# Queries and keys of the dilated attention by seven half-size products, its operands re-made in two forms, and its attention steps paced by hand

## The chip, the cores and the metric

The kernel runs on one core of one Trainium2 chip. The metric is the device time of one execution in microseconds, the median of three runs. PE is TensorE, DVE VectorE, ACT ScalarE, POOL GpSimd; SP is the sequencer whose queue issues most of the loads.

## The reference

One sequence of 512 tokens, width 1024, float32, goes through two layers and a final RMSNorm. Layer 0 attends in a window, layer 1 in three dilated groups of a window each; a SwiGLU feed-forward follows each attention. The change lies in layer 1:

```python
def dilated_mixture_attention(h, w_qkv, w_out):
    b, s, _ = h.shape
    qkv = (h @ w_qkv).reshape(b, s, N_GROUPS_B, 3, H_B, HEAD_DIM)      # 3 groups, q k v, 16 heads of 64
    slopes = alibi_slopes(H_B)[:, None]
    outs, lses = [], []
    for gi, (win, dil) in enumerate(DILATED_GROUPS):                    # (128,1), (512,4), (2048,16)
        q = to_residue(qkv[:, :, gi, 0], dil)[:, :, :, None]
        k = to_residue(qkv[:, :, gi, 1], dil)
        v = to_residue(qkv[:, :, gi, 2], dil)
        o, lse = banded_attention(q, k, v, slopes, dil, win // (2 * dil), BLOCK_B)
        outs.append(from_residue(o[:, :, :, 0], b, dil))
        lses.append(from_residue(lse[:, :, :, 0], b, dil))
    wts = jax.nn.softmax(jnp.stack(lses), axis=0)
    o = jnp.einsum('gbsh,gbshd->bshd', wts, jnp.stack(outs).astype(jnp.float32))
    return o.astype(h.dtype).reshape(b, s, H_B * HEAD_DIM) @ w_out

def reference(x, ...):
    for i in range(DEPTH):                                              # 2
        h = rmsnorm(x, norm_mix[i])
        x = x + (window_gqa_sink(h, ...) if i % 2 == 0 else dilated_mixture_attention(h, ...))
        h = rmsnorm(x, norm_ffn[i])
        x = x + swiglu(h, w_gate[i], w_up[i], w_down[i])
    return rmsnorm(x, norm_final)
```

## The kernel before

Activations lie transposed: `x` has 8 chunks of 128 features by 512 tokens. Every float32 operand of a product is kept as a high part (a copy rounded by ACT) and a low part (source less high part, by DVE), and a product is three matmuls: high by high, high by low, low by high (`mm3`, line 121). All matmuls of the dense parts move 256 columns against a 128x128 stationary block. "Step" is used here for six such matmuls, the unit in which the work is dealt out.

The two feed-forwards (`swiglu`, from line 601) compute most of their products in a Strassen-Winograd form already: a pair of weight blocks is combined into seven half-size products (`product`, line 737; `strassen`, line 744). Their weight sums are made by DMAs that add while they load (`load_sums`, line 690: two plain loads by SP, then two accumulating loads issued by POOL), two DVE additions and five splits.

The second attention (from line 1075) works on eight pairs of heads, p = 0 to 7.

- `qk_units` (line 1086) makes the queries and the keys of pair p in group g: two units of 8 steps each (`unit`, line 204). A unit loads one block of 128x1024 weights, splits it (ACT line 97, DVE line 98), runs 48 matmuls over all 512 tokens into one PSUM bank and leaves it scaled by DVE (`q_done` line 1093, `k_done` line 1107). The RMSNorm's row factor `rb` is applied here. For the first group the result is put from class order to token order, and split again for exact scores.
- `v_unit` (line 1121) makes the values of two pairs at a time: 16 steps (`values`, line 229). The values of group 0 for all pairs are made first, against `oh, ol`, which hold the input in token order; the rest runs against `xh, xl`, in class order.
- Per pair: `scores_a` (line 1139) for group 0 in two halves, with the reductions on DVE and the exponentials on ACT; `merge` (line 1281) takes the row statistics through DRAM into class order; `turn_a` (line 1173) transposes the weights on PE; then, in one go, `finish(p-1)` (the weighing of groups 1 and 2 of the pair before), `weigh_a`, and `scores_b` (line 1205) of groups 1 and 2; then exponentials (ACT), normalisation (DVE, and POOL line 1248), `turn_b` (line 1251) and `merge_rows` (line 1294).
- PE's order is written by hand: `attention_a` and `attention_b` give steps with waits between them, counted in the steps of a line of filling units (`fillers`, line 1377), and `spread` (line 169) deals them out. The order on DVE, ACT, POOL and SP in this stage is the planner's, which places instructions by program order, by readiness and by its own costs. Each engine then runs its list strictly in that order. Buffers of a tag rotate (`wraw`, `wh`, `wl`: 3 each, PSUM `mm`: 3, `sc`: 2, `tp`: 2, `ov`: 1), and a later tile of a tag waits for the last reader of the tile whose place it takes.

One filling line between two pairs holds 64 steps: six units of 8 and one `v_unit` of 16.

Of the kernel before, what the change touches and what calls it, by code (L numbers as in the profile page):

```python
# [53 lines left out]
def q_scales():  # L54

    s = np.zeros((128, 16), np.float32)
    for p in range(2):
        for i in range(4):
            for hf in range(2):
                s[64 * hf:64 * hf + 64, 4 * p + i] = 0.125 / SLOPES[8 * p + 4 * hf + i]  # L60
    for p in range(8):
        for hf in range(2):
            s[64 * hf:64 * hf + 64, 8 + p] = 0.125 / SLOPES[2 * p + hf]
    return s


def trunk(ctx, tc, xT, gains, sink, tabs, qsc, wunits, wv, outT, outR):
# [13 lines left out]
    x = const.tile([128, NK, S], F32, name="x")  # L81
    qs_sb = const.tile([128, 16], F32, name="qs_sb")
# [50 lines left out]
    def split_queries(q, pair):  # L133
        for a, (own, other) in enumerate((HALVES, HALVES[::-1])):
# [3 lines left out]
    def split_keys(k, pair, low):  # L138
        for a, (own, other) in enumerate((HALVES, HALVES[::-1])):
# [935 lines left out]
    with tc.tile_pool(name="l1", bufs=2) as pool:  # L1075
# [8 lines left out]
        dram = ctx.enter_context(tc.tile_pool(name="dram", bufs=2, space=bass.MemoryType.DRAM))  # L1084

        def qk_units(p, g):

            def views(out, *src):
                if g:
                    return (out, *src)  # L1090
                return (out.rearrange(IN_ORDER, m=16), *[t.rearrange(BY_CLASS, m=16) for t in src])

            def q_done(ps):
                name = "q1" if g else "qa"
                qk["q", p, g] = q = apart(pool, (p, g) > (0, 1) or not g,
                                          lambda: pool.tile([128, S], F32, name=name, bufs=2 if g else 1))
                out, src, rb = views(q, ps, norm["rb"])

                for to, at in ((slice(4, 32), slice(0, 28)), (slice(0, 4), slice(28, 32))) if g == 0 else [(slice(None),) * 2]:
                    nc.vector.scalar_tensor_tensor(out[..., to], src[..., at], qs_sb[:, 8 + p:9 + p], rb[..., at],  # L1100
                                                   op0=OP.mult, op1=OP.mult)
                if g == 0:
                    qk["qs", p] = apart(pool, p, lambda: [
                        pool.tile([128, S], F32R, name=f"qs{a}", bufs=1) for a in range(2)])
                    split_queries(q, qk["qs", p])

            def k_done(ps):
                name = "k1" if g else "ka"
                qk["k", p, g] = k = pool.tile([128, S], F32, name=name, bufs=2 if g else 1)
                out, src, rb = views(k, ps, norm["rb"])  # L1110
                nc.vector.tensor_tensor(out, src, rb, op=OP.mult)
                if g == 0:
                    qk["ks", p] = [pool.tile([128, S], F32R, name=f"ks{a}", bufs=1) for a in range(2)]
                    qk["kl", p] = [pool.tile([128, S], F32R, name=f"kl{a}", bufs=1) for a in range(2)]
                    split_keys(k, qk["ks", p], qk["kl", p])

            at = u1 + 6 * p + 2 * g
            return [lambda **kw: unit(at, xh, xl, "mm", q_done, **kw),
                    lambda **kw: unit(at + 1, xh, xl, "mm", k_done, **kw)]

        def v_unit(pg, g, **kw):
            if g == 0:
                vals[pg, 0] = v = pool.tile([128, 4, 256], F32, name="va", bufs=4)
                return values(1 + 3 * pg, 0, oh, ol, v, "mm mm mm mm" if pg else "ov sc tp mm")
# [372 lines left out]
```

## Time and profile before

| | |
|---|---|
| median of 3 runs | 1375.87 us (1375.38 to 1376.31) |
| the profiled execution | 1375.96 us, its span 1374.2 us |
| PE busy | 1361.4 us, 99%, 12246 matmuls and as many weight loads |
| DVE, ACT, POOL busy | 958.0 us (70%), 725.9 us (53%), 236.3 us (17%) |
| DMA | 164.63 MB, mean 120 GB/s |
| second attention | about 510 us to 1001 us of the span, the output projection after it to about 1038 us |

Busy shares are means over stages of different kinds; the stage in question is read by itself. Times in the profile count from the span's start. A line number with an engine names the operation's place in the kernel, sometimes in a helper (L97 and L98 are `split`, L126 is `mm3`, L741 the feed-forward's `product`).

### The profile page before, as it was taken

What the parts mean: (1) busy time and instruction counts of PE and PEld (TensorE: products, weight loads), DVE (VectorE), ACT (ScalarE), POOL (GpSimd) and SP (SyncE); (2) the same over time, 40 slices, a digit from 0 to 9 for tenths busy, and PEclk for the clock granted to TensorE, in tenths of its full rate; (3) what the DMA queues carried; (4) which work ended last, traced back from release to release, by engine and by line L of the source; (5) the groups of instructions that cost most, each with busy time, mean ns of one, the idle gap of its engine ahead of it and who ended that gap; (6) DMA issues with size and microseconds to landing.
All of it is one profiled execution on the core that took longest, in us unless ns stands there. A gap on an engine that the chain in (4) does not pass through costs nothing.

```text
span 1374.2 us, 29629 instructions
## 1 busy us (share of the span) xinstructions
PE 1361.4 (99%) x12246; PEld 1345.9 (98%) x12246; DVE 958.0 (70%) x1714; ACT 725.9 (53%) x1304; POOL 236.3 (17%) x339
## 2 busy tenths in 40 slices
PE   9999999999999999999999999999999999999997
PEld 9988999999999999999999999999999999999997
DVE  6876558877779986245655556646566887778985
ACT  6776534555555577344545436435344465555643
POOL 1234330122101000011111111211232022210204
PEclk9999999999999999999999999999999999999999
DMA  6110262787847332322222122222136287784821
GB/s 206 62 63 16 78 177 93 188 201 191 199 128 194 106 110 82 110 88 79 78 78 94 63 93 79 78 79 78 63 104 181 86 212 199 189 195 130 205 77 62
DMA packets 67111, 164.63 MB, mean 120 GB/s; under 512 B 8992, under 2 KB 11424, under 8 KB 66976
## 3 DMA queue, kind: packets, MB, share of 16 engines
q1 hardware_dynamic: 51904, 137.95, 30.7%
q0 software_dynamic: 14784, 24.27, 11.0%
q8 instruction: 96, 1.57, 0.5%
q10 hardware_dynamic: 288, 0.52, 0.1%
q14 instruction: 39, 0.32, 0.1%
HBM read 160.53 MB, written 2.17 MB: 118 GB/s over the span
## 4 chain that ended last, share of the span: by engine, by line
PE 93%; DVE 3%; ACT 2%; issue 1%; DMA 0%; POOL 0%; DVEq 0%; SPq 0%; ACTq 0%
PE mm L126 32%; PE mm L741 18%; PE sc L741 14%; PE psv L126 10%; PE tp L126 6%; PE sc L126 2%; PE ov L447 1%; PE ov L126 1%; PE sc L1216 1%; PE ovb L1271 1%; PE sc L1157 1%; PE tp L1179 1%; ACT pr L423 1%; PE mm L978 1%; DVE pr L416 1%; PE ov L1198 1%
## 5 line engine op out<-in xcount | busy, mean ns | idle before, releaser
L98 DVE TENSOR_TENSOR wl<-wraw,wh 128x1024 fp32r<-128x1024 f32 (+4 forms) x154 | 174.4, 1138 | 104.2 <-ACT wh L97 101.4
L126 PE MATMUL mm<-xh,wh 128*128 128x256 f32 x1120 | 225.9, 283 | 0.4 <-ACT xh L260 0.4
L126 PE MATMUL mm<-xl,wh 128*128 128x256 f32 x1120 | 219.6, 277 | 0.0
L126 PE MATMUL mm<-xh,wl 128*128 128x256 f32 x1120 | 219.3, 277 | 0.0
L97 ACT ACTIVATE wh<-wraw 128x1024 fp32r<-128x1024 f32 (+4 forms) x153 | 148.6, 981 | 126.9 <-PE mm L126 100.4
L126 PEld LDWEIGHTS mm<-xh,wh 128*128 128x128 f32 x1120 | 170.3, 189 | 2.3 <-issue 0.8
L126 PEld LDWEIGHTS mm<-xl,wh 128*128 128x128 f32 x1120 | 169.9, 189 | 0.3 <-DVE xl L261 0.3
L126 PEld LDWEIGHTS mm<-xh,wl 128*128 128x128 f32 x1120 | 169.7, 189 | 0.0
L697 POOL DMA_DIRECT2D w<-wunits x92 | 80.4, 907 | 445.9 <-DMA w<-wunits 121.7
L741 PE MATMUL mm<-bh,wh 128*128 128x256 f32 x368 | 101.6, 276 | 0.0
L741 PE MATMUL mm<-bl,wh 128*128 128x256 f32 x368 | 101.6, 276 | 0.0
L741 PE MATMUL mm<-bh,wl 128*128 128x256 f32 x368 | 101.6, 276 | 0.0
L741 PE MATMUL sc<-bh,wh 128*128 128x256 f32 x368 | 101.6, 276 | 0.0
L741 PE MATMUL sc<-bl,wh 128*128 128x256 f32 x368 | 101.6, 276 | 0.0
L741 PE MATMUL sc<-bh,wl 128*128 128x256 f32 x368 | 101.6, 276 | 0.0
L741 PE MATMUL mm<-bh,h 128*128 128x256 f32 x368 | 101.6, 276 | 0.0
L741 PE MATMUL mm<-bl,h 128*128 128x256 f32 x368 | 101.6, 276 | 0.0
L741 PE MATMUL mm<-bh,l 128*128 128x256 f32 x368 | 101.6, 276 | 0.0
L126 PE MATMUL psv<-wh,xh 128*128 128x256 f32 x288 | 80.5, 280 | 0.0
L126 PE MATMUL psv<-wl,xh 128*128 128x256 f32 x288 | 79.8, 277 | 0.2 <-DVE wl L98 0.2
L126 PE MATMUL psv<-wh,xl 128*128 128x256 f32 x288 | 79.7, 277 | 0.0
L1248 POOL TENSOR_SCALAR pr<-pr,mb 128x256 f32<-128x256 f32 x64 | 38.2, 611 | 183.0 <-DVE mb L1241 180.4
(256 smaller groups left out, 3952.9 us busy)
## 6 DMA issues: line engine op xcount, KB each, us to landing
wraw<-wunits SPq DMA_DIRECT2D x145, 512.0 KB, 3.3
w<-wunits SPq DMA_DIRECT2D x138, 256.0 KB, 3.9
w<-wunits POOLq DMA_DIRECT2D x92, 256.0 KB, 6.0
wraw<-wv SPq DMA_DIRECT2D x25, 512.0 KB, 3.5
wraw<-wunits SPq DMA_DIRECT2D x16, 384.0 KB, 5.0
x<-xT SPq DMA_DIRECT2D x8, 256.0 KB, 5.1
wraw<-wunits SPq DMA_DIRECT2D x3, 256.0 KB, 6.3
outT<-x SPq DMA_DIRECT2D x2, 384.0 KB, 2.8
```

The costliest lines, as they stand in the source:

```text
L97: nc.scalar.activation(out_h, src, AF.Copy)
L98: nc.vector.tensor_tensor(out_l, src, out_h.bitcast(F32), op=OP.subtract)
L126: nc.tensor.matmul(out[:, cols], a, b[:, cols], start=first and k == 0 and c == 0, stop=last and k == 2, skip_group_check=True)
L416: nc.vector.tensor_tensor_reduce(out=pr[:, e, :w], in0=ps[hf], in1=tab0[:, off:off + w], scale=SLOPES[heads[e]], scalar=-3e38, op0=OP.add, ...
L423: nc.scalar.activation(pr[:, e, :w + 1], pr[:, e, :w + 1], AF.Exp, bias=m[:, 1, e:e + 1], accum_out=m[:, 2, e:e + 1])
L447: nc.tensor.matmul(ov[64 * hf:64 * hf + 64, 256 * n:256 * n + 256], v0[:, k0 // 128 + kb, vs], st["pt", kb][:, 256 * hf:256 * hf + 256], s ...
L697: nc.gpsimd.dma_start(sums[:, 512 * k:512 * k + 512], v[:, 0:512], accum_op=OP.add)
L741: nc.tensor.matmul(out, a[:, j], b[:, j], start=first and j == 0 and i == 0, stop=j == 3 and i == 2, skip_group_check=True)
L978: nc.tensor.matmul(ps[:, 256 * h:256 * h + 256], a, (bl if low else bh)[:, slot, q % 4], start=q == 4 and k == 0 and 256 * h == cols.start ...
L1157: nc.tensor.matmul(out, qk["qs", p][a][:, 128 * t:128 * t + 128], kp[k], start=t == ts[0] and k == 0, stop=k == 1, skip_group_check=True)
L1179: nc.tensor.transpose(tp[:, (nb * a + kb) * 128:(nb * a + kb) * 128 + 128], st["pr", p, ts][:, a, o + 128 * kb:o + 128 * kb + 128], ident)
L1248: nc.gpsimd.tensor_scalar(of(pr[:, a, :], c), of(pr[:, a, :], c), den[:, c % 2, a:a + 1], 1.0, op0=OP.mult, op1=OP.mult)
```

## The change

1. Queries and keys of all pairs but the first (pair 0, group 0) are made together by `pair_unit`: a two by two block product of (weight rows in halves) by (query and key) against (token halves), as seven products of 12 matmuls, 14 steps where there were 16. The weights' sums are made as in the feed-forward. The products of a unit gather in two PSUM banks, a and b; four times in a unit a part of a bank is taken out by ACT or DVE before a later product adds to the same place.
2. The seven products need the input as it is and in four combinations. So `rb` is applied to the input once (`normed`), `xh, xl` are made anew from that, and the combinations (`summed`, `operand`) take the place of `oh, ol`.
3. The residual input `x` is written to DRAM (`kept_x`) and read back at the end (`x_back`); in its place lie single weight parts (`slots`) and one tile of values. The attention's results of pairs 0 to 5 go to DRAM (`kept_o`) and come back as `oh, ol` at the end (`back`, `back_split`).
4. The values of group 0 are made in front in the order of pairs 1, 2, 3, 0, with the halves of the weights in a new order (`ORDER`), so that the first half comes free after 12 of 16 steps. For the other groups values are taken out unscaled.
5. The steps of the attention stand at counted places (`usual`, `first`, `last`), exponentials and the rest of the normalisation as steps of their own; the transposes go in two groups, and both `turn_b` and `merge_rows` in one. `merge_rows` uses the bank `ov`.
6. Some buffers get fewer (`pt1` 8 to 7, `v1` 4 to 3, `va` 4 to 3, `mb` and `ew` 3 to 2, `acca` 2 to 1).

```diff
+        ORDER = [(0, 0), (0, 1), (1, 0), (1, 1), (2, 0), (3, 0), (2, 1), (3, 1)]
...
+        def pair_unit(p, g):
+            at = u1 + 6 * p + 2 * g
+            nqs = qs_sb[:, 16 + p:17 + p]
...
+            def sums():
+                s = t["sums"] = pool.tile([128, 1024], F32, name="w64", bufs=3)
+                nc.sync.dma_start(s[:, 0:512], wunits[at][:, 0:512])
+                nc.sync.dma_start(s[:, 512:1024], wunits[at + 1][:, 512:1024])
+                for k in range(2):
+                    nc.gpsimd.dma_start(s[:, 512 * k:512 * k + 512], wunits[at + 1][:, 0:512], accum_op=OP.add)
...
+            preps = [(-36, sums), (-18, raw), (-8, lambda: high((1, 2), "raw")), (-7, lambda: low((1, 2), "raw")),
+                     (-5, lambda: add(5)), (-4, lambda: high_one(5)), (-3, lambda: low_one(5)),
+                     (-2, lambda: high((6, 4), "sums")), (-1, lambda: low((6, 4), "sums")),
+                     (0, lambda: add(7)), (-2, last), (2, lambda: high_one(7)), (3, lambda: low_one(7)),
+                     (4, lambda: high_one(3)), (5, lambda: low_one(3))]
...
+            def product(m, key, cols, first, post):
+                def gen():
+                    if first:
+                        o[key] = bank("mm")
+                    (wh, wl), (bh, bl), out = w[m], against(m), o[key][:, cols]
+                    for j in range(4):
+                        for i, (a, b) in enumerate(((wh, bh), (wh, bl), (wl, bh))):
+                            nc.tensor.matmul(out, a[:, j], b[:, j], start=first and j == 0 and i == 0,
+                                             stop=j == 3 and i == 2, skip_group_check=True)
...
+            def copied(h):
+                nc.scalar.activation(o["gate"][:, (one, two)[h]], o["a"][:, one], AF.Copy, scale=nqs)
...
+            def done4():
+                nc.scalar.activation(half(o["second"], 1), src(o["b"][:, two]), AF.Copy)
+            def done6():
+                nc.vector.tensor_tensor(half(o["second"], 1), src(o["a"][:, one]), half(o["second"], 1), op=OP.add)
+            def done3():
+                nc.scalar.activation(half(o["second"], 0), src(o["a"][:, one]), AF.Copy)
+            def done7():
+                if g:
+                    nc.vector.scalar_tensor_tensor(o["first"], o["b"], nqs, o["first"], op0=OP.mult, op1=OP.add)
...
+            def products():
+                for gen in (product(1, "a", one, True, done1), product(2, "b", one, True, lambda: None),
+                            product(5, "a", one, False, lambda: copied(1)), product(4, "b", two, False, done4),
+                            product(6, "a", one, False, done6), product(7, "b", two, False, done7),
+                            product(3, "a", one, False, done3)):
+                    yield from gen
+            after = [] if g else list(zip((15, 16, 17, 19), parts(p)))
+            return 14, products(), preps + after
...
+        def taken(j):
+            nc.scalar.activation(of_class(raws[j]), x[:, j, :].rearrange(IN_ORDER, m=16), AF.Copy,
+                                 scale=g_sb[:, 2, j:j + 1])
+            nc.sync.dma_start(kept_x[j], x[:, j, :])
+        def normed(j):
+            nc.vector.tensor_tensor(raws[j], raws[j], norm["rb"], op=OP.mult)
+            split(xh[:, j, :], xl[:, j, :], raws[j])
...
+        periods = [[in_order_values(pg) for pg in (1, 2, 3, 0)]]
+        periods += [[vu(0, 1), pr_(0, 1), pr_(0, 2), pr_(1, 0), vu(0, 2)]]
+        periods += [[pr_(p, 1), pr_(p, 2), pr_(p + 1, 0), vu((p + 1) // 2, 2 - p % 2)]
+                    for p in range(1, 7)]
+        periods += [[pr_(7, 1), pr_(7, 2)]]
...
+        line = [(at, lambda j=j: taken(j)) for j, at in enumerate((2, 3, 4, 6, 7, 8, 10, 11))] + [(3, lambda: norm_rows(at=4))]
...
+        usual = {"a01": 1, "xa01": 4, "a23": 5, "xa23": 8, "merge": 9, "t01": 22, "t23": 30, "group": 43,
+                 "x01": 46, "x23": 48, "r01": 50, "r23": 52, "back": 58}
+        first = {"t01": 30, "t23": 40, "group": 59, "x01": 62, "x23": 64, "r01": 66, "r23": 68, "back": 74}
+        last = {"a01": 1, "xa01": 4, "a23": 5, "xa23": 8, "merge": 9, "t01": 16, "t23": 21, "group": 28}
...
+        x_back()
+        spread([lambda: [back_split(c) for c in range(4, 6)], steps["x01"], 2, steps["x23"], 2, steps["r01"],
+                1, steps["r23"], 6, steps["back"], 5, lambda: finish(7), 3], fill)
```

Places in `preps` count steps from the unit's own first step; places in `usual`, `first` and `last` count steps from the start of the pair's period. The period of pair p (1 to 6) has 58 steps: three pair units of 14 and one value unit of 16.

More of the change, by code (lines that the diff above doesn't have):

```diff
@@ new lines, in v_unit, with loads, halves, gen @@
+        def v_unit(pg, g):
+            w, t = [], {}
+            def loads():
+                t["raw"] = [weight_tiles() for k in range(2)]
+                for k in range(2):
+                    nc.sync.dma_start(t["raw"][k][0], wv[2 * (1 + 3 * pg + g) + k])
+            def halves(k):
+                raw, wh, wl = t["raw"][k][0], *[z[:, 96:1120] for z in t["raw"][k][1:]]
+                split(wh, wl, raw)
+                w.append(chunks(t["raw"][k], (4, 256), 96))
+            def gen():
+                vals[pg, g] = v = pool.tile([128, 4, 256], F32, name="v1", bufs=3)
+                yield from v_products(xh, xl, w, v, ["mm"] * 4, lambda b: 1.0)
+            return 16, gen(), [(-9, loads), (-6, lambda: halves(0)), (-3 if g == 2 or pg else -4, lambda: halves(1))]
@@ new lines, in operand, with vu @@
+        def operand(j):
+            split(oh[:, j, :], ol[:, j, :], raws[j])
+        def vu(pg, g):
+            return v_unit(pg, g)
+        pr_ = pair_unit
+        periods = [[in_order_values(pg) for pg in (1, 2, 3, 0)]]
[3 more added lines that the diff above has]
+        periods += [[pr_(7, 1), pr_(7, 2)]]
+        counts = [sum(unit[0] for unit in units) for units in periods]
@@ new lines, in trunk, with back, back_split @@
+        out_line = [plain_unit(j, lo, hi) for lo, hi in ((0, 6), (6, 7)) for j in range(3)]
+        fill = lined([unit for units in periods for unit in units] + out_line)
+        def back():
+            for c in range(3):
+                kept = pool.tile([128, 2, S], F32, name="w64", bufs=3)
+                for k in range(2):
+                    nc.sync.dma_start(kept[:, k, :], kept_o[2 * c + k])
+                st["kept", c] = kept
+        def back_split(c):
+            split(oh[:, c, :], ol[:, c, :], st["kept", c // 2][:, c % 2, :])
@@ new lines, in x_back @@
+        def x_back():
+            nonlocal x
+            x = stream()
+            for j in range(NK):
+                nc.sync.dma_start(x[:, j, :], kept_x[j])
+        steps = attention(0)
+        line = [(at, lambda j=j: taken(j)) for j, at in enumerate((2, 3, 4, 6, 7, 8, 10, 11))] + [(3, lambda: norm_rows(at=4))]
+        line += [(17, steps["a01"]), (20, steps["xa01"]), (33, steps["a23"]), (36, steps["xa23"]), (42, steps["merge"])]
+        line += [(at, lambda j=j: normed(j)) for j, at in enumerate((20, 22, 24, 26, 35, 37, 39, 41))]
@@ L1396, in trunk @@
         for p in range(8):
             if p:
-                spread(attention_a(p), fill)
-            else:
-                spread(firsts[6:], fill)
-                spread([1], fill)
-            first, second, rows = attention_b(p)
-            if p < 7:
-                spread([15, first, 16, second, rows, 1], fill)
-        spread([9, first, 5, second, rows, 2, lambda: finish(7)], fill)
-        spread([3], fill)
+                steps = attention(p)
+            ats = first if p == 0 else usual if p < 7 else last
```

332 lines of the change are left out of this document (232 added, 100 removed).

## The prediction

> **What bounds the kernel now.** First the page: busy shares and the chain that ended last.
>
> ```profile
> span 1374.2 us, 29629 instructions
> PE 1361.4 (99%) x12246; PEld 1345.9 (98%) x12246; DVE 958.0 (70%) x1714; ACT 725.9 (53%) x1304; POOL 236.3 (17%) x339
> PE 93%; DVE 3%; ACT 2%; issue 1%; DMA 0%; POOL 0%; DVEq 0%; SPq 0%; ACTq 0%
> ```
>
> PE is the bound and almost all of the chain. Whether it waits anywhere is told by the view of waits on PE; its two longest rows, and the only one for a weight of values:
>
> ```profile
> PE ssq L278 <- ACT tmp L271: 1.5, 1, 1.5
> PE warm L335 <- POOL ident masks.py:199: 1.4, 1, 1.4
> ...
> PE psv L126 <- DVE wl L98: 0.2, 1, 0.2
> ```
>
> So a matmul taken away shortens the kernel by its pitch, as long as the others keep up. The pitch and the course of a pair's period stand in the chain in order of time (start, duration, what), here from two windows:
>
> ```profile
> 497.77 1.36 PE sc L741 x12
> ...
> 655.75 1.90 PE ovb L1271 x32
> ...
> 659.20 1.99 PE sc L1216 x32
> 661.18 10.42 PE mm L126 x90
> ...
> 709.69 1.90 PE ovb L1271 x32
> ```
>
> Twelve matmuls of a feed-forward product take 1.36 us, 113.3 ns each, each with weights of its own; a step of six is 0.68 us. From one weighing to the next, 655.75 to 709.69, a period is 53.9 us. Last, the engines by stage (busy us of PE, PEld, DVE, ACT, POOL, then clock, DMA share, GB/s): the start of the values, a later part of them, a period, the tail, and a stretch of the second feed-forward.
>
> ```profile
> 522.70:533.60 10.90, 10.90 (x99) 10.90 (x98) 7.58 (x13) 8.51 (x15) 0.00 (x0) 1.00 0.45 147
> 545.50:556.40 10.90, 10.90 (x98) 10.90 (x98) 3.76 (x12) 4.83 (x14) 2.40 (x4) 1.00 0.31 99
> 661.20:715.10 53.90, 53.90 (x523) 53.48 (x523) 31.30 (x79) 26.26 (x60) 8.45 (x14) 1.00 0.24 80
> 984.14:1001.00 16.86, 16.86 (x160) 16.42 (x160) 8.49 (x29) 6.08 (x21) 3.93 (x8) 1.00 0.01 2
> 1250.00:1300.00 50.00, 50.00 (x444) 50.00 (x443) 46.49 (x60) 27.25 (x38) 7.04 (x8) 1.00 0.58 151
> ```
>
> In a period DVE is busy 58% and ACT 49%, PE always; in the feed-forward PE is full beside a DVE at 93%, there in an order written by hand.
>
> **The change, term by term.**
>
> *Matmuls.* A pair unit has 7 x 12 = 84 where two units had 96. Units made so: three in the period of pair 0, three in each of the next six, two in the last: 23. Gone are 23 x 12 = 276 matmuls x 113.3 ns = **-31.3 us**. Everything else on PE (values, scores, transposes, projection) keeps its count. Bringing the transposes together saves a few changes between groups; I take nothing for it.
>
> *Work added to DVE and ACT.* Rows by form (busy us, mean ns of one):
>
> ```profile
> L98 DVE TENSOR_TENSOR wl<-wraw,wh 128x1024 fp32r<-128x1024 f32 x124 | 153.5, 1239 | 97.4 <-ACT wh L97 96.7 <-issue 0.3
> L97 ACT ACTIVATE wh<-wraw 128x1024 fp32r<-128x1024 f32 x124 | 130.4, 1056 | 123.4 <-PE mm L126 97.3 <-issue 13.6 <-PE psv L126 9.8
> L720 DVE TENSOR_TENSOR l<-w,h 128x512 fp32r<-128x512 f32 x46 | 31.5, 686 | 1.0 <-ACT h L714 0.9
> L724 DVE TENSOR_TENSOR wraw<-w,wraw 128x512 f32<-128x512 f32 x46 | 31.8, 691 | 1.4
> L714 ACT ACTIVATE h<-w 128x512 fp32r<-128x512 f32 x46 | 29.0, 630 | 17.4 <-PE mm L741 9.9 <-DMA w<-wunits 4.3 <-issue 3.0
> L753 ACT ACTIVATE gs<-mm 128x256 f32<-128x256 f32 x92 | 35.0, 380 | 44.1 <-PE mm L741 42.3
> L764 DVE TENSOR_TENSOR us<-sc,us 128x256 f32<-128x256 f32 x46 | 19.2, 418 | 0.0
> L1236 ACT ACTIVATE pr<-pr,mb 128x256 f32<-128x256 f32 x64 | 31.7, 496 | 17.1 <-DVE mb L1232 17.1
> ```
>
> Both forms split two 1024-wide tiles. A pair unit adds three 512-wide splits and two 512-wide sums: DVE 3 x 0.686 + 2 x 0.691 = 3.4 us, ACT 3 x 0.63 = 1.9 us. Taking the results out costs DVE one 512-wide and one 256-wide pass where it had two 512-wide: about -0.3. ACT gains four copies of 256: 1.5. Three units: DVE +9.3, ACT +10.2 a period; the split of the attention's result (line 98, one 512-wide on each) leaves for pairs 0 to 5, -0.7 and -0.6. A period becomes 53.9 - 3 x 1.36 = 49.8 us, DVE 31.3 + 8.6 = 39.9 (80%), ACT 26.3 + 9.6 = 35.9 (72%). Neither is the bound, and 93% was borne above. These cost nothing in the mean; what they do to single waits comes next.
>
> *DMA.* A unit loaded 2 x 512 KB; now 512 (raw), 512 (sums), 512 (added on top, POOL's queue), 256 (last): 0.8 MB more, three a period, and 0.26 MB of kept results. With 80 GB/s x 53.9 us = 4.3 MB before, that is about 7 MB in 49.8 us, 140 GB/s, below the 151 quoted. The accumulating loads are issued 36 steps, 24 us, ahead. POOL's list then holds them beside the statistics and the normalisation: an accumulating load that waits for SP's load holds up what stands behind it. Nothing, but see the tail.
>
> *Handoffs inside a unit: the main unknown.* Product 5 adds to the place from which ACT has just to copy product 1; one product lies between. The same for product 5's result before 6, 4's before 7 (ACT), and 6's before 3 (DVE): four in a unit, 92 in all. How fast such a handoff is, from the timeline:
>
> ```profile
> 1129.61 0.28 PE L741 MATMUL mm<-bh,l 128*128 128x256 f32 x1
> 1129.92 0.38 ACT L753 ACTIVATE gs<-mm 128x256 f32<-128x256 f32 x1 [0.84 <-PE mm L741]
> ```
>
> The product's last matmul ends at 1129.89, the copy starts 0.03 later and takes 0.38. The window from that end to product 5's first matmul is 1.36 - 0.28 + 0.11 = 1.19 us. So about 0.7 us of lateness is free. A 1.05 us split that started just before the product's end uses 1.05 and costs 0.34 at worst; a 0.63 one costs nothing. Two 1024-wide splits in a unit's 14 steps (9.5 us on PE) are on the engine 22% of the time, a third of that in the harmful part, at half of 0.34 in the mean: 0.22 x 0.32 x 0.17 = 0.01 us. The exponentials (0.5 each) come four in a row, and the planner may put a batch ahead of a copy; DVE's handoff, one in four, meets splits of 1.24. So I take 0.03 a handoff, 92 x 0.03 = **+2.8 us** (0 to 0.34 each: 0 to 31).
>
> *Scores.* The second half reuses the banks of the first, four steps on:
>
> ```profile
> 685.19 0.91 PE sc L1157 x8
> ...
> 688.81 0.91 PE sc L1157 x8
> 686.18 0.27 DVE L1165 CUSTOM_DVE_ANT_0 pr<-sc,tab 64x128 f32<-64x128 f32 x1
> ...
> 688.32 0.17 DVE L1168 TENSOR_SCALAR sta<-mx 128x2 f32<-128x2 f32 x1
> ```
>
> DVE came late (it was splitting) and was done at 688.49, 0.3 us ahead of PE. The step distance stays four, and `back`, a 1024-wide split and a sum now stand just before. A lateness of one 512-wide operation more costs 0.4. I take 0.2 in seven periods: **+1.4 us** (0 to 7).
>
> *Front.* `taken` puts eight ACT passes into the first 11 steps. Such passes took 0.64 each:
>
> ```profile
> 511.06 2.56 ACT L260 ACTIVATE oh<-x,g_sb 128x512 fp32r<-128x512 f32 x4
> 532.77 1.06 ACT L97 ACTIVATE wh<-wraw 128x1024 fp32r<-128x1024 f32 x1
> ```
>
> 5.1 us against 2.4 us free in 522.70:533.60, so ACT is 2.7 us over. Behind it stands the split of the second value unit's later half (532.77 before); the new order of halves frees its buffer two steps, 1.4 us, earlier, and 0.3 us was left. The stall lies between 0 (the split goes ahead of the copies) and 2.7; **+0.5 us**. The passes of `normed` and `summed` come later, where (545.50:556.40) DVE is busy 3.8 and ACT 4.8 of 10.9 us: nothing.
>
> *Tail.* `back` of the last pair stands 11 steps, 7.5 us, after the scores, where its first half stood 9 and its second 14. POOL's normalisation ends that chain:
>
> ```profile
> 982.15 1.99 PE sc L1216 x32
> 987.96 1.96 POOL L1248 TENSOR_SCALAR pr<-pr,mb 128x256 f32<-128x256 f32 x4 [17.56 <-DVE mb L1241]
> 990.34 1.97 POOL L1248 TENSOR_SCALAR pr<-pr,mb 128x256 f32<-128x256 f32 x4 [0.42 <-DVE mb L1241]
> 667.37 2.94 POOL L1248 TENSOR_SCALAR pr<-pr,mb 128x256 f32<-128x256 f32 x4 [0.42 <-ACT wh L97]
> 668.59 1.38 DVE L98 TENSOR_TENSOR wl<-wraw,wh 128x1024 fp32r<-128x1024 f32 x1
> ```
>
> It ends 992.31 - 984.14 = 8.2 us after the scores; PE wants it at 7.5 + 0.4. With two re-made splits (line 98) on DVE just ahead: **+0.8 us** (0.3 to 2.3). The read-back of `x` (2 MB) waits for the last product and stands on SP's queue with the projection's weights; the first residual comes 18 steps and more, 12 us, later, and 2 MB at 200 GB/s are 10: nothing, 0 to 4 if a weight stands behind it.
>
> The last two rows show four POOL passes at 2.94 us while DVE subtracted, against 1.96. The Trainium skill, "SBUF — State Buffer", section "Who interferes with whom", says that a DVE instruction with two SBUF inputs contends with a GpSimd instruction that reads SBUF. The rows agree (2.94 to 1.96, and 1.38 on DVE against 1.24). It speaks against the change, which adds just such subtractions: with both fours slowed the chain would be 10.1 us, still inside a usual period's 15 steps (10.2), in the tail 2.2 us late, and the sum 1.4 us more.
>
> Sum: -31.3 + 2.8 + 1.4 + 0.5 + 0.8 = -25.8. From the profiled execution's 1375.96 us (span 1374.2 and 1.8 around it; 0.1 over the median): **1350.2 us**. This case lies between 1344.7 (no stall) and 1355 (handoffs as taken, scores, front, tail and read-back at half their upper ends: 2.8 + 3.5 + 1.4 + 1.2 + 2 = 10.9).
>
> **Rivals.**
>
> *Half lost in handoffs.* The planner puts exponentials or splits before the copies in many units: 0.15 us in each of 92, 13.8 us, a score wait of 0.5 in seven periods, 3.5, front and tail as above: 1344.7 + 18.6 = 1363. For it: both engines are a third busier, and every handoff is met by a fixed list. Against: PE waits for neither now. Span of this case 1355 to 1373.
>
> *Slower: a handoff behind two operations.* At 0.34 us a handoff, one whole 1024-wide split ahead of each copy, 92 x 0.34 = 31.3 us and the gain is gone. With a 0.38 us copy more ahead of a third of them, 31 x 0.38 = 12 us: 1388. For it: strict lists. Against: a unit has two such splits for its four handoffs, so it must come from batches or a list that runs late throughout.
>
> *The cut is none.* If a matmul with new weights each time cost more than one of a couple on the same weights, 84 could cost as much as 96 (129 ns): 1376. The row of 12 at 1.36 us, just such products, speaks against it; only other addresses could bring it.
>
> **How the numbers follow.** The forecast 0.60, half lost 0.26, slower 0.09, no cut 0.05. Within 0.2% (2.8 us, about what a measurement tells from no change) lie a part of "no cut" and a sliver of both neighbours: faster 0.87, same 0.04, slower 0.09. The range reaches from 1344 to 1366, holding the first case and most of the second, a little over 8 in 10.
>
> **What would show it.** 11970 matmuls; 1.36 us for every product; a period of about 50 us. PE's waits: rows for copies and `done6` short or none (half lost: 10 us and more there). DVE near 80%, ACT near 72% in a period, 140 GB/s. One wait for a value weight near the front, one for POOL's `pr` in the tail. Wrong would be a pitch over 113 ns, PE waiting for sums or slots, or waits of PE above 10 us.

## The result, and the profile after

The changed kernel takes 1357.5 us, median of 4 runs (1356.9 to 1357.9), beside 1376.1 (1375.4 to 1377.3) for the kernel before in the same session: a ratio of 0.9864, 95% interval 0.9847 to 0.9881, 18.6 us less. The forecast was 1350.2, so 7.3 us that the sum promised did not come. The profiled executions differ by 1374.2 - 1356.1 = 18.1 us of span, and the removed matmuls alone were 31.3; the account below looks for 13.2 us.

The head of the page after:

```profile
span 1356.1 us, 29792 instructions
PE 1340.4 (99%) x11970; PEld 1321.3 (97%) x11970; DVE 1039.2 (77%) x1869; ACT 812.6 (60%) x1489; POOL 277.7 (20%) x385
```

The count of matmuls is the forecast one. PE is busy 99% of the span: what is missing is not idle time, except for a few us. The groups by line and shape (count, busy us, mean ns of one):

```profile
L761 PE MATMUL mm<-bh,wh 128*128 128x256 f32 x368 | 101.6, 276 | 0.0
...
L1272 PE MATMUL mm<-oh,slots 128*128 128x256 f32 x368 | 72.9, 280 | 0.0
```

A matmul's duration in these rows is its distance to the next one and about 163 ns (276 beside 113), so 276 against 280 ns says that the pair units' matmuls (line 1272) stand 4 ns further apart than the feed-forward's (line 761), with the same shape and the same precision. The chain shows how, piece by piece (start, us, what; the last number counts matmuls):

```profile
636.95 11.97 PE mm L1272 x102
...
668.73 1.99 PE sc L1435 x32
670.71 10.43 PE psv L144 x90
681.14 0.92 PE tp L1482 x7
682.06 0.02 issue
682.08 0.33 PE tp L1482
...
684.45 2.72 PE mm L1272 x24
...
688.08 11.62 PE mm L1272 x102
...
721.10 10.80 PE psv L144 x90
...
734.88 2.83 PE mm L1272 x24
```

The same 24 matmuls take 2.72 us (113.3 ns each) in one period and 2.83 (117.9) in the next, the same 90 take 10.43 and 10.80. The rows of waits further down name nothing in these pieces. In the starts of the single matmuls the distances are either 113, 113, 114 or 117, 118, 118. I call the second kind locked. Over 113.3 ns each, the locked matmuls between 522 and 1019 us cost 7.4 us; in the same stage before they cost 1.0.

In most runs of matmuls it settles in the first five behind a seam (transposes, scores, weighing: 120, 117, 116, 114, 113 or 117, 118, 118, 118) which kind they are, and that holds to the next seam. But a lock can also begin inside a run. The 102 matmuls at 688.08 take 11.62 us, those at 636.95 take 11.97, and the latter change from one kind to the other at one matmul (ACT, then PE's weight loads, then the matmuls):

```profile
637.72 0.62 ACT L1242 ACTIVATE slots<-wraw 128x512 fp32r<-128x512 f32 x1
638.24 0.45 ACT L1287 ACTIVATE q<-mm,qs_sb 128x256 f32<-128x256 f32 x1
...
638.60 0.19 PEld L1272 LDWEIGHTS mm<-oh,wl 128*128 128x128 f32 x1
638.75 0.19 PEld L1272 LDWEIGHTS mm<-oh,wh 128*128 128x128 f32 x1
...
638.82 0.31 PE L1272 MATMUL mm<-oh,wh 128*128 128x256 f32 x1
638.97 0.28 PE L1272 MATMUL mm<-ol,wh 128*128 128x256 f32 x1
```

The matmul at 638.82 is the first of product 6, and its weight load waits for ACT's copy of product 5's result (line 1287), which stood behind a split. The load begins 0.15 us after the one before it instead of 0.11, the distance between the matmuls becomes 149 ns, and the 82 behind it are locked. In the seven pair units that the scores interrupt, this load came late five times, by 0.03 to 0.04 us, and four times a locked run followed: 1.3 of the 7.4 us.

PE's waits, first in the front, then from there to the end of the attention (engine, line, for whom: us in total, times, longest):

```profile
PE psv L144 <- ACT wh L115: 1.0, 1, 1.0
PE psv L144 <- DVE wl L116: 0.9, 1, 0.9
PE rrow L331 <- DVE rstd L315: 0.2, 1, 0.2
...
PE tp L1482 <- POOL pr L1470: 0.4, 1, 0.4
```

So no product waits long for a copy or for `done6`, no score for its bank, and no residual for the read-back; waits as short as the one at 638.75 are not in these rows. What waits in the front is the first value unit's second half. ACT's timeline there, and the windows (us, busy PE, PEld, DVE, ACT, POOL; granted clock; DMA share; GB/s):

```profile
518.28 2.29 ACT L1624 ACTIVATE k<-xa,g_sb 128x512 f32<-128x512 f32 x2
520.47 2.28 ACT L1624 ACTIVATE q<-xb,g_sb 128x512 f32<-128x512 f32 x2
522.66 1.17 ACT L1624 ACTIVATE v<-xb,g_sb 128x512 f32<-128x512 f32 x1
523.73 1.04 ACT L115 ACTIVATE wh<-wraw 128x1024 fp32r<-128x1024 f32 x1
524.79 1.28 ACT L311 ACT_TABLE_LOAD   x1
```

```profile
524.50:527.00 2.50, 1.24 (x6) 0.83 (x6) 1.80 (x5) 2.47 (x4) 0.00 (x0) 0.97 1.09 231
527.00:530.60 3.60, 3.41 (x17) 3.42 (x18) 0.72 (x2) 3.60 (x6) 0.00 (x0) 0.55 1.09 271
665.20:715.60 50.40, 50.35 (x487) 49.45 (x487) 38.76 (x93) 35.06 (x81) 13.91 (x20) 1.00 0.57 148
```

Five passes of `taken` (line 1624) ran before the split of the second half and before the norm's root. PE stood still twice, for 1.0 and 0.9 us, and then ran 3.6 us at a granted clock of 0.55. The 330 matmuls from the first value unit on took 41.85 us, where the same 330 took 37.53 before. The third row is a whole period: 50.4 us for a forecast of 49.8, when its locked stretches are few (others took 51.2).

Last, POOL's normalisation in the period whose chain stands above:

```profile
676.70 1.96 POOL L1470 TENSOR_SCALAR pr<-pr,mb 128x256 f32<-128x256 f32 x4 [20.86 <-DVE mb L1463]
679.08 2.94 POOL L1470 TENSOR_SCALAR pr<-pr,mb 128x256 f32<-128x256 f32 x4 [0.41 <-DVE mb L1463]
```

POOL ends at 682.02, and the eighth transpose (line 1482) begins at 682.08. From the first of the eight to what follows, the transposes take 0.89 us where nothing holds them (three periods, all behind locked values, which brought PE there later), 1.23 to 1.69 elsewhere: 2.3 us more over eight periods, 0.8 of it in the first.

The account: 31.3 - 6.4 (locked matmuls, 7.4 less 1.0) - 4.3 (front: 3.7 in matmuls over 123 ns, the half clock among them, and 0.6 at the norm's rows) - 2.3 (transposes) = 18.3, against 18.1. It is a sum of readings of one trace; no run takes the locks away.

### The profile page after: what moved, and what is told of

It reads as the page before. It is cut to its first block, busy times and chain, and to the rows that moved or that the text cites. A ratio compares the mean times of both kernels' runs of the same rounds, so it can differ in the third digit from the quotient of the medians.

```text
span 1356.1 us, 29792 instructions
## 1 busy us (share of the span) xinstructions
PE 1340.4 (99%) x11970; PEld 1321.3 (97%) x11970; DVE 1039.2 (77%) x1869; ACT 812.6 (60%) x1489; POOL 277.7 (20%) x385
## 4 chain that ended last, share of the span: by engine, by line
PE 90%; ACT 5%; DVE 3%; issue 1%; SPq 0%; DMA 0%; POOL 0%; DVEq 0%; ACTq 0%; POOLq 0%
PE mm L761 18%; PE mm L1272 17%; PE sc L761 14%; PE mm L144 12%; PE psv L144 9%; PE tp L144 6%; PE sc L144 2%; PE ov L467 1%; PE ov L144 1%; PE ovb L1495 1%; PE sc L1369 1%; PE sc L1435 1%; PE tp L1397 1%; ACT pr L443 1%; DVE pr L436 1%
## 5 line engine op out<-in xcount | busy, mean ns | idle before, releaser
L116 DVE TENSOR_TENSOR wl<-wraw,wh 128x1024 fp32r<-128x1024 f32 (+4 forms) x108 | 118.1, 1103 | 37.7 <-ACT wh L115 35.0
L115 ACT ACTIVATE wh<-wraw 128x1024 fp32r<-128x1024 f32 (+4 forms) x107 | 100.2, 948 | 61.4 <-PE mm L144 39.2
L144 PE MATMUL mm<-xh,wh 128*128 128x256 f32 x384 | 77.5, 283 | 0.4 <-ACT xh L280 0.4
L144 PE MATMUL mm<-xl,wh 128*128 128x256 f32 x384 | 75.5, 278 | 0.6 <-DVE xl L281 0.6
L144 PE MATMUL mm<-xh,wl 128*128 128x256 f32 x384 | 75.5, 278 | 0.0
L1272 PE MATMUL mm<-oh,slots 128*128 128x256 f32 x368 | 72.9, 280 | 0.0
L761 PEld LDWEIGHTS mm<-bl,wh 128*128 128x128 f32 x368 | 69.1, 188 | 0.0
L761 PEld LDWEIGHTS mm<-bh,wl 128*128 128x128 f32 x368 | 69.1, 188 | 0.0
```

The costliest lines, as they stand in the source:

```text
L115: nc.scalar.activation(out_h, src, AF.Copy)
L116: nc.vector.tensor_tensor(out_l, src, out_h.bitcast(F32), op=OP.subtract)
L144: nc.tensor.matmul(out[:, cols], a, b[:, cols], start=first and k == 0 and c == 0, stop=last and k == 2, skip_group_check=True)
L761: nc.tensor.matmul(out, a[:, j], b[:, j], start=first and j == 0 and i == 0, stop=j == 3 and i == 2, skip_group_check=True)
L1272: nc.tensor.matmul(out, a[:, j], b[:, j], start=first and j == 0 and i == 0, stop=j == 3 and i == 2, skip_group_check=True)
```

## Experiments

Three causes were to be tried: the pitch, the front, the transposes. In all kernels below PE's order is that of the changed kernel unless it is said. A run of matmuls behind a seam counts as locked where the median distance of its 6th to 20th matmul is 116.5 ns or more; the excess is the sum over 113.3 ns of distances of 115 to 123 ns, from 522 us to 1019 us. A lock that begins at product 6 is in the excess and not in the counts.

### e1_again: the same kernel once more

> The changed kernel as it is, once more. Two theories for the matmuls of 117.8 ns that stand in stretches between 500 and 1019 us (7.4 us over 113.3 ns each, against about 1.0 us before): set by what the program fixes (order and addresses), or by chance at each seam. Fixed: the stretches begin and end at the same matmuls again (733.2 to 750.4 and 721.3 to 731.5 slow, 686 to 699 and 767 to 790 quick) and the sum is 7.4 within 0.5 us. Chance: about half of the stretches are others and the sum is off by 1 to 3 us. Both: 1357.5 within 1 us.

1357.3 us (1356.7 to 1360.6), ratio 0.9869 (0.9854 to 0.9884); the profiled execution is the longest of the four, 1360.6. The excess is 9.0 us and other stretches are locked: of the pairs of heads 0 to 6, it was 2, 5 and 6 that locked behind their scores and now 5 alone; behind the norm-row step (line 1525) it was 2 and 5 and now 0, 4, 5 and 6. So something that the program does not fix picks the stretch, and the theory that the program fixes it fell. The share by kind of seam moved less: behind the first groups' transposes (line 1397) 10 of 16 locked both times. Of the 1.6 us more, 1.3 are in the output projection, which locked here at a break of 0.3 us and stayed so for over 300 matmuls.

Product 6 came late three times (distances of 153 to 206 ns), and each time a locked run followed. Seven profiles have the changed kernel's order with all operands on 64 bytes: the first one, this one, and those of e1_shift64, e1_rotate, e3_dummy_pad, e3_halves and e3_gated3 below. In them product 6 came late in all 37 units that were not locked up to there and in none of the 12 that were, and 27 of the 37 were locked behind it. That the late load starts the lock is read from its place; no run removes it.

The windows of the front in this execution:

```profile
524.50:527.00 2.50, 0.80 (x4) 0.60 (x5) 1.40 (x2) 2.47 (x4) 0.00 (x0) 1.00 1.03 166
527.00:530.60 3.60, 3.35 (x30) 3.15 (x29) 0.60 (x5) 3.60 (x5) 0.00 (x0) 1.00 1.08 276
```

The same waits, and here no half clock; PE lost the time later instead (0.5 and 0.7 us at 539 and 552), since ACT's list was as late as before. So the half clock of the first profile cost little of its own: the 330 matmuls took 41.61 us here and 41.85 there. The Trainium skill, "TensorE: Matmul & The Clock Gate", section "What's actually happening", says that the gate watches a free-running window, so that it depends on where in it one lands; the two executions agree.

### e1_shift64 and e1_rotate: other addresses for the pair units' weights

```diff
-[wpool.tile([128, 1024], F32R, name=n) for n in ("wh", "wl")]
+[wpool.tile([128, 1152], F32R, name=n)[:, 64:1088] for n in ("wh", "wl")]      # shift64
-        steps = attention(0)
+        steps, _ = attention(0), [wpool.tile([128, 1152], F32R, name=n) for n in ("wh", "wl")]   # rotate
```

> The hi and lo tiles of the pair units' weights (products 1, 2, 4, 6) lie 256 bytes further into the places they already have; every instruction and its order stay. If the distance between the addresses of the two operands sets the pitch, the slow stretches of the pair units change as a whole: their excess of about 6 us falls under 2 or rises over 10, and the time goes by 4 us or more one way. If the addresses have no part, the stretches stay at the same matmuls and the time is 1357.5 within 1 us. If chance sets it, some stretches are others, and the time is within 2 us.

> One unused hi and one unused lo tile are taken at the start of the second attention, so every later weight of it lies in the next of the three places; order and instructions stay. If the address of the weights sets the pitch, the slow seams behind the norm-row step of heads 2 and 5 (733 and 886 us) turn quick and those of two other heads (0, 3, 6 or 1, 4, 7) turn slow, with a sum of 5 to 9 us. If not, heads 2 and 5 stay slow, and the time is 1357.5 within 1 us.

1357.8 us (ratio 0.9866, 0.9852 to 0.9881) and 1358.3 (0.9871, 0.9856 to 0.9886). Excess 6.2 and 6.6 us, behind line 1397 11 and 9 of 16 locked, behind line 1525 1 and 0 of 7, where the two profiles of the changed kernel had 2 and 4. The pairs that the rotation should have locked (0, 3, 6 or 1, 4, 7) did not. Neither the third of three buffers nor 256 bytes more matter. 256 bytes are a multiple of 128, so the distance between the operands modulo 128, which the last experiment points at, is the same here.

### e1_gated, e2_gated_again, e2_dummy, e3_dummy_pad: 32 bytes

e1_gated was meant for the front. It makes the passes' gains from the norm's root, in a new tile:

```diff
+        gated = spool.tile([128, NK], F32, name="gated", bufs=1)
+        nc.vector.scalar_tensor_tensor(gated, norm["r"], 0.0, g_sb[:, 2, :], op0=OP.mult, op1=OP.add)
...
-                                 scale=g_sb[:, 2, j:j + 1])
+                                 scale=gated[:, j:j + 1])
```

> The scale of the eight passes that carry x to the other layout is made from the reciprocal root of the norm (times zero, plus the gains), so they cannot run before it; one DVE instruction of 8 columns more. Theory of the front: the five early passes (5.7 us of ACT) hold up the split of the first value unit's second half and the norm's root, which cost about 2.5 us of PE's waits and then 1.8 us of half clock, so 1357.5 becomes about 1353.0 and the granted clock stays over 0.95 there. Rival: the second half waits for its own transfer, or the norm's chain is late anyway; then the waits move by under 1 us and the time is 1356.5 to 1357.5. A second rival: the passes only move to where va, the norm's rows and the queries' splits are wanted, and PE waits there; 1356 to 1360.

1391.4 us, slower than the kernel before (ratio 1.0111, 1.0095 to 1.0128): no theory had that. The feed-forward, which the edit does not touch, ran at 117 to 118 ns. The same kernel again:

> The kernel of e1_gated as it is, which took 1391.4 us because most of its matmuls, in stages that the edit does not touch too, ran at 117 to 118 ns (14.0 us over 113.3 ns each before 535 us, 10.7 us in the last stage). If the program fixes that (its instructions and where they lie), it is 1391 again within 1 us with the same stretches. If loading it onto the chip fixes it anew, it is somewhere between 1353 and 1391, with other stretches.

1391.9: the program fixes it. The next kernel keeps the tile and the instruction and leaves the passes as they were:

> The changed kernel with the one small DVE instruction of e1_gated and with nothing that waits for it: the passes stay as they were. If the layout of the program sets the pitch, one instruction more can do it: over 1375, with matmuls at 117 to 118 ns from the start on. If the late passes did it (through what they delay), it is 1357.5 within 1 us, with a sum of 7 to 9 us over 113.3 ns behind 520 us and under 2 us before. Chance anew at each loading would give either.

1387.4 us (1.0082, 1.0067 to 1.0097). The passes had no part in it. In the built program the new tile of 32 bytes had moved `oh`, `ol` and all that lies behind them from 0 to 32 modulo 64. So the last of these puts the instruction's output into the unused tile `align_xh`, and no address moves:

```diff
-        gated = spool.tile([128, NK], F32, name="gated", bufs=1)
+        gated = spare[:, 0:NK]          # spare: the tile "align_xh"
```

> The instruction of e2_dummy, its 32 bytes of output now in a tile of 96 bytes that the changed kernel has and does not use, so that no address moves. In e2_dummy the new tile of 32 bytes had moved oh, ol and all that lies behind them to addresses that are 32 modulo 64, and matmuls whose moving operand lies so took 118.3 ns on the mean, 96% of them over 116. If the address does it: 1357.5 within 1.5 us, under 2.5 us over 113.3 ns before 520 us. If the instruction did it: 1387 again.

1359.8 us (0.9881, 0.9866 to 0.9896), 0.8 us over what was expected for the address; before 522 us the excess is 1.4, behind it 8.1. One group of the feed-forward in e2_dummy:

```profile
L761 PE MATMUL mm<-bh,wh 128*128 128x256 f32 x368 | 103.4, 281 | 0.0
```

and in e3_dummy_pad:

```profile
L761 PE MATMUL mm<-bh,wh 128*128 128x256 f32 x368 | 101.6, 276 | 0.0
```

The address did it: 27.7 us for 32 bytes. The trace of e2_dummy has a control of its own: the value products against `xh` and `xl`, whose operands did not move, stayed at 113.6 to 113.8 ns. That changed the question about the changed kernel, where all these operands lie on 64 already.

### e3_halves: where the sums go

```diff
-                    (wh, wl), (bh, bl), out = w[m], against(m), o[key][:, cols]
+                    (wh, wl), (bh, bl), out = w[m], against(m), [o[key][:, c] for c in (cols, (one, two)[cols == one])]
...
-                            nc.tensor.matmul(out, a[:, j], b[:, j], start=first and j == 0 and i == 0,
+                            nc.tensor.matmul(out[(j + i) % 2], a[:, j], b[:, j], start=first and j == 0 and i < 2,
```

> Every second matmul of the pair units' products adds into the other half of its PSUM bank (so queries and keys are not the reference's); order, operands and waits stay. All matmul operands of the changed kernel lie on multiples of 64 bytes, and still 19 of some 45 runs of matmuls lock at 117.8 ns from the seam on, 10 of 16 behind the first groups' transposes, where in the kernel before, whose 512-wide products alternate between the halves, none of 32 locks. If adding into the same half matmul after matmul is what allows the lock: at most 2 of 16 behind those transposes, the excess of the pair units falls from 5 to under 1 us, and the time to 1352 to 1354. If not: 8 to 12 of 16 again and 1357.5 within 1.5 us.

1359.7 us (0.988, 0.9865 to 0.9894), 0.7 us over what was expected for no effect, 11 of 16 locked behind line 1397, excess 7.2 us. The theory fell: the locks came as before when the matmuls alternated between the halves of a bank.

### The front: e1_gated, e2_pool, e3_gated3

In e1_gated all eight passes stood behind the root. The early waits were gone; PE's waits from 520 to 640 us of its second run:

```profile
PE psv L144 <- ACT wh L115: 2.9, 1, 2.9
PE psv L144 <- DVE wl L116: 1.0, 1, 1.0
PE sc L1369 <- ACT va L1181: 0.9, 1, 0.9
```

The 2.9 lie 15 us behind the first value unit's start, at the second value unit's split: the second rival. e2_pool put the passes on POOL (it has the 32 bytes too: 1398.8 us, 1.0165, 1.0148 to 1.0182):

> The eight passes go from ACT to POOL, behind POOL's copy of the summed squares (the same small DVE instruction, made from that copy). Theory of the front: with ACT free of their 8.8 us, the second half's split runs at once, PE's waits at 524 to 527 us (about 2.5 us) and the half clock behind them (1.8 us) go: 1353 if the pitch is as in the changed kernel. Rival: the norm's root, not the split, holds PE, and the gain is under 1 us: 1357. If the pitch goes slow as in e1_gated the sum is 1385 to 1390, and the front is read from the trace alone: no wait over 0.6 us between 521 and 535, clock over 0.95.

```profile
PE psv L144 <- DVE qa L1122: 7.6, 1, 7.6
PE sc L1369 <- ACT ks L161: 1.6, 1, 1.6
```

The early waits went here too, and PE waits 7.6 us further on. POOL takes 2.0 to 3.3 us a pass, and ACT's list has a split into `slots` behind them, which lies where `x` was: ACT idled 16.3 us until POOL had read `x`, with the norm's rows queued behind. e3_gated3 moved no address, and let three passes run early:

```diff
-                                 scale=g_sb[:, 2, j:j + 1])
+                                 scale=(g_sb[:, 2] if j < 3 else gated)[:, j:j + 1])
```

> Three of the eight passes may run early as now; the other five wait for the norm's root (their gains are made from it, into the unused tile, so no address moves). Front theory: ACT reaches the second half's split at 521.7 instead of 523.7 and the root at 522.7 instead of 524.8, so PE's two waits of 1.3 us at 524.8 and 526.1 shrink to under 0.6 in sum and the half clock behind them (1.8 us) goes; against it the five passes stand before the second value unit's split, worth a wait of up to 2 us there: 1353 to 1356. Rival: the passes cost the same wherever they stand on ACT, since ACT is full from 515 to 545: 1357 to 1358, with the wait at the second value unit as in e1_gated (2.9 us).

1358.8 us (0.9874, 0.9857 to 0.989). PE's waits from 515 to 560 us, and ACT:

```profile
PE psv L144 <- ACT wh L115: 1.2, 1, 1.2
PE psv L144 <- DVE wl L116: 0.9, 1, 0.9
PE rrow L331 <- DVE rstd L315: 0.3, 1, 0.3
```

```profile
534.88 2.34 ACT L1627 ACTIVATE v<-xb,align_xh 128x512 f32<-128x512 f32 x2
537.09 0.48 ACT L1181 ACTIVATE va<-psv,rstd 128x256 f32<-128x256 f32 x1
537.45 1.07 ACT L115 ACTIVATE wh<-wraw 128x1024 fp32r<-128x1024 f32 x1
```

The rows of waits read as in the changed kernel, but they now lie at 537 us, not at 525: two passes, 2.34 us together, stand ahead of the next split. In the 330 matmuls from the first value unit on, distances over 240 ns cost 3.0 us here and 3.1 in the changed kernel. With the half clock and the short breaks counted, all 330 took 41.22 us here and 41.85 and 41.61 in the changed kernel's two profiles: 0.4 to 0.6 us less, where 2 to 4 were hoped for, and the time shows nothing of it. The rival holds in the main: in both places on ACT that were tried, the planner has some passes ahead of a split that PE wants.

### e2_group41: the second groups' scores two steps earlier

```diff
-        usual = {..., "group": 43, "x01": 46, "x23": 48, "r01": 50, "r23": 52, "back": 58}
+        usual = {..., "group": 41, "x01": 44, "x23": 46, "r01": 48, "r23": 50, "back": 58}
```

> In the usual periods the scores of the second groups and all that follows them up to POOL's normalisation come two steps of the line earlier (41, 44, 46, 48, 50 for 43, 46, 48, 50, 52); the transposes stay at 58. Theory: these transposes took 1.23 to 1.69 us for 0.89 in five of eight periods because POOL's second four instructions end after PE is there; two steps are 2.7 us, so all take 0.89 and the time falls by 1.5 to 2.3 us, to 1355 to 1356. Rival: the chain sticks on ACT or DVE all the same (value copies and splits stand between its exponentials), and under 0.5 us comes. The pitch may hide either; the durations of the transposes are read from the trace.

1364.4 us (0.9917, 0.9903 to 0.9932), 7 slower than the changed kernel. (Two steps of 0.68 us are 1.4 us; the 2.7 of the expectation is a slip.) POOL ahead of the transposes of one period, and a row of PE's waits that is new:

```profile
778.42 2.49 POOL L1470 TENSOR_SCALAR pr<-pr,mb 128x256 f32<-128x256 f32 x4 [19.25 <-DVE mb L1463]
782.83 2.96 POOL L1470 TENSOR_SCALAR pr<-pr,mb 128x256 f32<-128x256 f32 x4 [1.92 <-ACT ks L160]
```

```profile
PE mm L1272 <- ACT q L1287: 2.0, 6, 0.4
```

The rival came, and more. Earlier in the line, the scores met the splits of keys on ACT, which the planner put between the exponentials; POOL's second four began 2 us behind its first four instead of 0.4, and the transposes of the usual periods took 1.22 to 1.35 us. PE's eighth transpose again starts 0.06 us behind POOL's end (785.85, 785.79), so POOL is what holds them; that an earlier POOL would free them is not shown. The row of waits is a handoff inside the pair unit, the copy of line 1287 again, now late by 0.33 us six times. These 2.0 us and 1.2 more in the transposes are half of the 6.2 us by which the profiled spans differ; the rest was not traced. The seams changed as well: where scores are now followed by pair units, 6 of 6 locked.

### e4_both: all on 128 bytes, passes on two engines

```diff
-    const.tile([128, 96], F32, name="align_x")
+    const.tile([128, 32], F32, name="align_x")
-    const.tile([128, 24], F32, name="align_xh")
+    spare = const.tile([128, 40], F32, name="align_xh")
...
+    const.tile([128, 16], F32, name="align_wh")
+    spool.tile([128, 16], F32, name="align_oh", bufs=1)
...
+        late = [spare[:, 8 * k:8 * k + 8] for k in range(2)]     # gains: [0] from POOL's copy, [1] from the root
...
+            if j < 3:
+                nc.gpsimd.tensor_scalar(of_class(raws[j]), src, late[0][:, j:j + 1], None, op0=OP.mult)
+            else:
+                nc.scalar.activation(of_class(raws[j]), src, AF.Copy, scale=late[1][:, j:j + 1])
```

> Two edits in two places that the trace keeps apart. First, xh, xl, oh, ol and the weights' tiles all begin on multiples of 128 bytes (in the changed kernel xh, xl, oh and ol are 64 modulo 128, and the quick seams behind scores are those whose moving operand, the weights, is on 128). If 128 bytes decide the lock: at most 2 of 16 seams behind the first groups' transposes lock, for 9 to 14 of 16 in all runs so far, and 4 to 5 us go. If what follows the seam decides it (the pair unit's order of operands, not addresses): 8 to 14 of 16 again and nothing goes. Second, three of the eight passes go to POOL behind its copy of the summed squares and five stay on ACT behind the norm's root. If the 8.8 us of ACT are the price of the front: PE's waits over 0.15 us between 521 and 552 us (4.3 us in all in the changed kernel, 3.7 with five passes late and three early on ACT) fall to 1 to 2, and 2 to 3 us go. If other work of ACT or DVE stands in line there: 3.5 again. So: 1351 with both, 1355 with the second alone, 1353 with the first alone, 1358 with neither.

1404.4 us (1.0204, 1.019 to 1.0218), the slowest of all. Neither 128-byte theory had it. The feed-forward's group and pieces of the chain in one period:

```profile
L763 PE MATMUL mm<-bh,wl 128*128 128x256 f32 x368 | 104.1, 283 | 0.0
```

```profile
694.65 10.99 PE psv L146 x90
...
712.37 12.17 PE mm L1274 x102
```

By the mark of 116.5 ns all 16 seams behind the transposes lock, and all 8 behind scores that values follow. The edit moved `xh`, `xl`, `oh` and `ol` from 64 to 0 modulo 128 and left the weights at 0, so the distance between the operands changed with it, and this kernel can't tell what 128 bytes do at the old distance. The feed-forward is the clean comparison, since its products are the same in every kernel. By the start addresses in the built program and the distances in the trace:

| feed-forward products (line 761, weights `wh`, `wl`) | moving, stationary mod 128 | mean ns | at 116 or more |
|---|---|---|---|
| changed kernel | 64, 0 | 113.0 to 113.8 | 0% |
| e2_dummy | 96, 0 | 118.1 to 118.5 | 94 to 98% |
| e4_both | 0, 0 | 119.9 to 120.0 | 100% |

So the pitch changes with the places where the operands start, and of these three pairs 64 and 0 is the good one. The distance alone isn't the rule: in e4_both the products of line 763 whose operands do lie 64 apart (0 and 64) ran at 117.4 to 118.4 ns, and in e2_dummy those at 96 and 32 at 117.4 to 118.3, as locked stretches do. The passes: PE's waits in the front were 1.1, 0.9 and 0.6 us, and distances over 240 ns cost 3.4 us, at 544 and 557. Three passes less on ACT did not help, since its last two, 2.3 us, again stood ahead of the second value unit's split.

No kernel here beats the changed one.

## Why the prediction was right, and what its sum missed

- *Matmuls, -31.3 us.* Right in count (11970). The size supposed 113.3 ns throughout. 24 matmuls took 2.72 us in some places and 2.83 in others; the step that failed is the pitch, which the prediction took from one row of twelve and called safe ("only other addresses could bring it"). 6.4 us. Addresses can indeed bring it, and 27.7 us of it, but they are not what did it here: the changed kernel's operands lie as those of the kernel before.
- *Handoffs inside a unit, +2.8 (0 to 31).* 0.2 us by themselves: five of the 92 came 0.03 to 0.04 us late. The bound was much too wide, but the 0.7 us of free lateness was a little too: the copy of line 1287 took 0.45 to 0.47 us for 0.38, and what waits is the weight load, about 0.1 us ahead of its matmul. Behind four of the five stands a locked run, 1.3 us, counted under the pitch. e2_group41 shows a copy that is late by more: 0.33 us.
- *Scores, +1.4.* 0.
- *Front, +0.5 (0 to 2.7).* 4.3 us. The mechanism, `taken` crowding ACT, was right; the size of a pass was off (1.16 to 1.19 us for 0.64), and so was the place: five passes ran ahead of the first value unit's second half and of the norm's root, not only ahead of the second unit. The row used for 0.64 reads `x` in its own order. `taken` reads it in steps of 16 elements, as a pass of the kernel before did just behind that row:

  ```profile
  513.52 1.22 ACT L260 ACTIVATE xh<-x,g_sb 128x512 fp32r<-128x512 f32 x1
  ```

  The Trainium skill, "SBUF — State Buffer", section "Door 1: The DMA port swizzle", notes that accesses that cross to a new 16-byte line pay; the passes agree, and this row, of a pass over the same order, was the one to take.
- *Tail, +0.8, usual periods 0.* It was the other way round: the tail's transposes cost 0.34 us, the first period's 0.80 and those of the usual periods 1.2. The chain from the end of the scores to POOL's end was reckoned as 8.2 us, 10.1 with both fours slowed, inside 15 steps of 10.2; in the period shown it took 11.3 (670.72 to 682.02), and 15 steps 10.4. The second four ran at 2.94 us, as the row and the rule in the prediction had it; the first stayed at 1.96, and ACT and DVE were later than assumed.
- *Read-back of `x`.* 0.
- *Luck.* 1357.5 lies in the range, but 2.5 us outside the span of the forecast's own case (1344.7 to 1355) and inside that of "half lost in handoffs". The handoffs and scores that the sum put at 4.2 us came to 0.2; that offset a third of the 11.7 us that it lacked or had too small (pitch 6.4, front 3.8, transposes 1.5). That the matmuls go and PE stays the bound was right; that the sum ended within 7.3 us is in part luck.
- *Rivals.* "Half lost in handoffs" gave 1363, near in size, wrong in place. "The cut is none" named the pitch and asked too much of it.
- *What would show it.* Period, load (DVE 77%, ACT 70% in the quoted period, 148 GB/s) and waits came as told. The test "a pitch over 113 ns" fired.

What stays open: why pair units lock more often. Behind the same transposes 0 of 32 runs locked before, where 512-wide products followed, and 9 to 14 of 16 in every kernel here with the addresses kept. Weights' buffers, 256 bytes, and the half of the bank are excluded. The order in which a product's twelve matmuls take their operands does not do it alone: the feed-forward's products take them in the same order, with starts at 64 and 0 as well, and none of them locks (113.0 to 113.8 ns). That order behind a seam wasn't tried by itself; nor was a pair unit whose product 6 is never late, nor a kernel without the passes.

## What to carry to other kernels

Price removed matmuls by the stretch that they leave behind, not by the best row of one: look for two pitches of the same shape in the chain, and let the difference times the stage's matmuls be an end of the range (here 4.6 ns times the 3516 such matmuls of the stage, 16 us). Before adding a tile, however small, look at what its bytes do to the start addresses of matmul operands behind it. And price a pass by a row that walks the tensor in the same order; when it is put on a full engine, ask which item of that list PE wants next, since moving it may do little more than choose whom it delays (here 0.4 to 0.6 us).

## What the runs showed of the hardware

- 32 bytes in front of the operands cost 27.7 us in 1387.4, through matmuls that have nothing to do with the added instruction; putting both operands on 128 bytes brought 119.9 to 120.0 ns in the feed-forward for 113.0 to 113.8.
- With the good addresses a run of matmuls still falls into one of two pitches, 113.3 or 117.9 ns, within five matmuls of a seam, or changes to the slow one where a weight load came 0.03 us or more late (27 of 37 times), and holds it to the next seam, once for over 300 matmuls. Two executions of one program choose differently (excess 7.4 and 9.0 us).
- Two waits of 1.0 and 0.9 us, one matmul apart, were followed by a clock of 0.55 for 3.6 us in one execution of a program and by 1.00 in another.
